# Inverse deviations of the four norms: from chains of small DVE operations to a power operation and a Newton step on Pool

## The chip, the core and the metric

The kernel runs on one core of a Trainium2 chip. The metric is the device time of one execution in microseconds. The core's engines are named as in the profile: PE (matrix multiply; PEld is its weight load), DVE (vector), ACT (scalar, activation functions), POOL (GpSimd), and SP, which here issues DMAs.

## The reference

One decoder layer over 320 tokens: 256 of a prompt and 8 sequences of 8 new tokens each. Cut to what matters:

```python
h = rms_norm(x, norm_mix)                       # norm 1
u, q, k, v, g = split(h @ w_in)
s5_out = s5_mixer(u, ...)                       # complex diagonal state, scanned over positions
o = retention(rotary(q), rotary(k), v, ...)     # 8 heads of 128 channels
mu, var = mean(o, -1), mean(square(o - mu), -1)
o = (o - mu) * rsqrt(var + 1e-6)                # group norm, per head and token
x = x + concat([s5_out, silu(g) * o * ret_gn_w]) @ w_out
h2 = rms_norm(x, norm_ffn)                      # norm 2
x = x + (silu(gate(h2)) * up(h2)) @ w_ffn_out
y = rms_norm(x, norm_final)                     # norm 3
```

`rms_norm` is `x * rsqrt(mean(x * x) + 1e-6) * g`. Outputs are `y` and the new states of both mixers.

## The kernel before

Activations lie with channels on the 128 partitions and the 320 tokens along the row. Every weight tile of 128x1024 is loaded by SP (`raw`), rounded by ACT (`hi`, L128) and its remainder formed by DVE (`lo`, L129), each with three buffers in the mixer; every product is three matmuls of 128x320 (L139 to L141). The norms' scale isn't applied to the matmul's input: the products are taken with the unscaled `x`, and the scale of each token, broadcast to all partitions as `rbc`, is multiplied in when the products leave PSUM.

Three of the four norms go through `rstd_bcast` (L191). PE sums squares over the partitions into `ps_r`, one column for each of three stretches of 128 tokens; DVE brings the sums into `ms` (128x3); `rsqrt` (L181) makes the inverse root `y` of them; and PE broadcasts it with three matmuls against the identity (`ps_r<-ident,ry`, L216), from which ACT copies `rbc`. In norm 1 ACT also copies `ry` itself to `rtok`. In norm 3 PE is kept busy with matmuls on ones (`warm_ps`) during the chain. `rsqrt` was ten DVE operations: a first guess from the bits of the number, then three Newton steps of three operations.

The group norm is in `head_v` (L644): DVE takes mean and variance of `po` in PSUM (`bn_stats`, `bn_aggr`, into `mv` of 128x2x4), then one operation for the variance, the ten of `rsqrt`, and one for the shift: `gy`, scale and shift for four stretches of tokens. ACT applies them to `po` (`on`, L680), and PE transposes `on` into `pn` a while later; in between PE has other matmuls.

The order of work is set in two ways. DVE, ACT and SP are ordered by a scheduler that sees priorities and dependences. PE and Pool are in `manual_schedule`: their instructions stand in the order in which the Python code issues them. That order comes from generators on a model clock: `spawn` puts one in a heap with a due time, `run_due` runs those that are due between matmuls.

What stands on Pool early is the S5 mixer's part: `s5_params` computes step sizes, sines and cosines on DVE (scratch `cl`, result `ecs`), then Pool writes the rotation tables `tab` from `ecs` by doubling, for channel group 0 at once (`s5_tables`, L456) and for groups 1 to 3 as spawned generators. DVE goes on with powers and factors (`lp`, `ff`, `gp`, at last `lx`, all through scratch in `cl`), after which two MEMSETs on Pool clear the two `cl` tiles (L447), since chunks of the mixer use them next. Only after `s5_params` has been issued comes `finish_norm` (L836), which runs `rstd_bcast` for norm 1 in two parts: sums and `rsqrt` first, the broadcast a model delay later, in the midst of the matmuls of head 0's `v`.

## Time and profile before

| what | us |
|---|---|
| median of 3 runs | 1490.53 (1490.41 to 1491.65) |
| the profiled execution's own time | 1490.19 |
| its span, first to last instruction | 1488.4 |
| PE busy | 1462.0 |
| DVE busy | 865.4 |
| ACT busy | 615.1 |
| POOL busy | 77.1 |

In the profile a row of a timeline gives the start in the span, the duration, engine, line, operation and output<-inputs; brackets give how long the engine had been idle before, and what ended that. Where several like instructions follow each other, they are one row (x3) with the time from the first's start to the last's end. A row of the waits gives engine and line, who released it, the total in us, the number of times and the longest. A row of groups gives, after the bar, busy us and the mean ns of one. A row of windows gives the stretch, its length, the busy time in it, granted clock and DMA.

### The profile page before, as it was taken

The page shows a single profiled execution, that of the slowest core. Times are in us where ns is not written, and L with a number is a line of the kernel's source. Part 1 is how long each engine was busy: PE and PEld are TensorE (multiplying, and loading weights), DVE is VectorE, ACT ScalarE, POOL GpSimd, SP SyncE. Part 2 cuts the span into 40 slices and gives each one's busy share as a digit, 9 for nine tenths or more (in the row PEclk, how much of TensorE's full clock was granted, in tenths as well). Part 3 has the DMA queues.
Part 4 walks back from the last instruction along what each step waited for, and adds up shares of the span by engine and source line. Part 5 has one row for each costly group of instructions (what it writes and reads, how often), then busy time and mean ns, then how long its engine had stood idle before and what let it go on. Part 6 is the DMA issues. An engine that isn't in the chain of part 4 may idle for free.

```text
span 1488.4 us, 26179 instructions
## 1 busy us (share of the span) xinstructions
PE 1462.0 (98%) x10558; PEld 1443.7 (97%) x10558; DVE 865.4 (58%) x1507; ACT 615.1 (41%) x980; POOL 77.1 (5%) x159
## 2 busy tenths in 40 slices
PE   9999999999999999999999999999999999999996
PEld 8989999898999999999999999999999999999996
DVE  7988777675746765655444444444444454444454
ACT  6555554554425543333333333333333333333352
POOL 1395000000000000000000000000000000000001
PEclk9999999999999999999999999999999999999999
DMA  7443443433554466665444355444445544445443
GB/s 270 149 140 123 142 142 114 136 121 114 191 163 146 152 210 188 215 221 185 149 149 153 119 155 166 159 149 149 139 137 152 172 153 149 149 123 156 150 145 108
DMA packets 79752, 230.79 MB, mean 155 GB/s; under 512 B 15248, under 2 KB 27664, under 8 KB 79632
## 3 DMA queue, kind: packets, MB, share of 16 engines
q1 hardware_dynamic: 79488, 229.09, 48.2%
q8 instruction: 83, 1.36, 0.4%
q14 instruction: 37, 0.30, 0.1%
q10 hardware_dynamic: 144, 0.04, 0.0%
HBM read 218.04 MB, written 7.63 MB: 152 GB/s over the span
## 4 chain that ended last, share of the span: by engine, by line
PE 68%; DVE 1%; ACT 0%; issue 0%; DVEq 0%
PE ps_fo L139 7%; PE ps_fu L139 7%; PE ps_fu L141 7%; PE ps_fo L140 7%; PE ps_fu L140 7%; PE ps_fo L141 7%; PE ps_fg L139 7%; PE ps_fg L141 7%; PE ps_fg L140 7%; PE ps_o L139 1%; PE ps_o L140 1%; PE ps_o L141 1%; PE ps_g L140 1%; PE ps_g L141 1%; PE ps_g L139 1%; DVE x L174 0%
## 5 line engine op out<-in xcount | busy, mean ns | idle before, releaser
L129 DVE TENSOR_TENSOR lo<-raw,hi 128x1024 fp32r<-128x1024 f32 (+1 forms) x420 | 472.1, 1125 | 393.6 <-ACT hi L128 392.6
L128 ACT CAST hi<-raw 128x1024 fp32r<-128x1024 f32 (+1 forms) x420 | 407.4, 970 | 704.0 <-PE ps_fo L140 188.8
L139 PE MATMUL ps_fg<-hhi,hi 128*128 128x320 f32 x704 | 217.5, 309 | 0.0
L140 PE MATMUL ps_fo<-alo,hi 128*128 128x320 f32 x704 | 217.5, 309 | 0.0
L141 PE MATMUL ps_fo<-ahi,lo 128*128 128x320 f32 x704 | 217.5, 309 | 0.0
L139 PE MATMUL ps_fo<-ahi,hi 128*128 128x320 f32 x704 | 217.5, 309 | 0.0
L141 PE MATMUL ps_fg<-hhi,lo 128*128 128x320 f32 x704 | 217.4, 309 | 0.0
L140 PE MATMUL ps_fu<-hlo,hi 128*128 128x320 f32 x704 | 217.4, 309 | 0.0
L139 PE MATMUL ps_fu<-hhi,hi 128*128 128x320 f32 x704 | 217.4, 309 | 0.0
L141 PE MATMUL ps_fu<-hhi,lo 128*128 128x320 f32 x704 | 217.4, 309 | 0.0
L140 PE MATMUL ps_fg<-hlo,hi 128*128 128x320 f32 x704 | 217.3, 309 | 0.0
L139 PE MATMUL ps_p<-xhi,hi 128*128 128x320 f32 x576 | 183.6, 319 | 0.0
L141 PE MATMUL ps_p<-xhi,lo 128*128 128x320 f32 x576 | 177.9, 309 | 0.0
L140 PE MATMUL ps_p<-xlo,hi 128*128 128x320 f32 x576 | 177.8, 309 | 0.0
L140 PEld LDWEIGHTS ps_fg<-hlo,hi 128*128 128x128 f32 x704 | 132.4, 188 | 0.3
L139 PEld LDWEIGHTS ps_fg<-hhi,hi 128*128 128x128 f32 x704 | 132.3, 188 | 0.3
L139 PEld LDWEIGHTS ps_fo<-ahi,hi 128*128 128x128 f32 x704 | 132.4, 188 | 0.0
L140 PEld LDWEIGHTS ps_fu<-hlo,hi 128*128 128x128 f32 x704 | 132.4, 188 | 0.0
L141 PEld LDWEIGHTS ps_fo<-ahi,lo 128*128 128x128 f32 x704 | 132.4, 188 | 0.0
L141 PEld LDWEIGHTS ps_fg<-hhi,lo 128*128 128x128 f32 x704 | 132.4, 188 | 0.0
L139 PEld LDWEIGHTS ps_fu<-hhi,hi 128*128 128x128 f32 x704 | 132.4, 188 | 0.0
L141 PEld LDWEIGHTS ps_fu<-hhi,lo 128*128 128x128 f32 x704 | 132.4, 188 | 0.0
(414 smaller groups left out, 2003.4 us busy)
## 6 DMA issues: line engine op xcount, KB each, us to landing
raw<-w_fi SPq DMA_DIRECT2D x176, 512.0 KB, 3.7
raw<-w_in SPq DMA_DIRECT2D x76, 512.0 KB, 3.8
raw<-w_fo SPq DMA_DIRECT2D x64, 512.0 KB, 3.5
raw<-w_out SPq DMA_DIRECT2D x32, 512.0 KB, 3.7
raw<-w_fo SPq DMA_DIRECT2D x64, 192.0 KB, 2.4
rt<-r SPq DMA_DIRECT2D x8, 512.0 KB, 4.7
raw<-w_glu SPq DMA_DIRECT2D x8, 512.0 KB, 3.6
raw<-r SPq DMA_DIRECT2D x8, 512.0 KB, 4.4
```

Of the source, the lines that this page charges most:

```text
L128: act.copy(hi[:, :m], raw[:, :m])
L129: dve.tensor_tensor(lo[:, :m], raw[:, :m], f(hi[:, :m]), SUB)
L139: pe.matmul(ps, hi, xhi[:, k], start=k == 0, stop=False)
L140: pe.matmul(ps, hi, xlo[:, k], start=False, stop=False)
L141: pe.matmul(ps, lo, xhi[:, k], start=False, stop=k == nk - 1)
```

## The change

`rsqrt` becomes five Pool operations on the same small tiles: a power (exponent -0.5, from a constant tile `mhalf` filled by a MEMSET at the start), and one Newton step of four. It now takes the variance itself and not its half with a minus sign, so `ms` is scaled by 1/D instead of -0.5/D; that operation stays on DVE. In the group norm the two operations around `rsqrt` go to Pool too and become three: the mean's sign, the addition of epsilon, and the shift. They stand outside the block of high priority now. Per head DVE has 12 operations fewer and Pool 8 more; per norm it is 10 and 5.

```diff
+    mhalf = cst.tile([P, 4], F32, name="mhalf")
+    pool.memset(mhalf, -0.5)
...
     def rsqrt(t, y, tmp):
 
-        ts(y.bitcast(I32), t.bitcast(I32), -0.5, MUL, float(0x1EF759DF), ADD)
-        for _ in range(3):
-            tt(tmp, y, y, MUL)
-            tt(tmp, tmp, t, MUL)
-            stt(y, tmp, 1.5, y, ADD, MUL)
+        pool.tensor_tensor(y, t, mhalf[:, 0:t.shape[1]], ALU.pow)
+        pool.tensor_tensor(tmp, y, y, MUL)
+        pool.tensor_tensor(tmp, tmp, t, MUL)
+        pool.tensor_scalar(tmp, tmp, -0.5, 1.5, MUL, ADD)
+        pool.tensor_tensor(y, y, tmp, MUL)
...
-            ts(ms, ps, -0.5 / D, MUL, -0.5 * EPS, ADD)
+            ts(ms, ps, 1.0 / D, MUL, EPS, ADD)
             if last is not None:
-                stt(ms, sums(last(), "ps_l"), -0.5 / D, ms, MUL, ADD)
+                stt(ms, sums(last(), "ps_l"), 1.0 / D, ms, MUL, ADD)
...
-            ts(mv[:, 1], mv[:, 1], -0.5, MUL, -0.5 * EPS, ADD)
-            rsqrt(mv[:, 1], y[:, 0], y[:, 1])
-            stt(y[:, 1], mv[:, 0], -1.0, y[:, 0], MUL, MUL)
+        pool.tensor_scalar(mv[:, 0], mv[:, 0], -1.0, None, MUL)
+        pool.tensor_scalar(mv[:, 1], mv[:, 1], EPS, None, ADD)
+        rsqrt(mv[:, 1], y[:, 0], y[:, 1])
+        pool.tensor_tensor(y[:, 1], mv[:, 0], y[:, 0], MUL)
```

PE's instructions stand in the same order as before. On Pool, at the end of the first tables, stood before (in brackets the engines whose semaphores an instruction waits for; line numbers are of the kernel before):

```order
L477 TENSOR_TENSOR tab<-tab,ecs 128x8x32
L478 TENSOR_TENSOR tab<-tab,ta 128x8x32 [waits Pool_49]
L447 MEMSET cl_131 128x1280 [waits DVE_49]
L447 MEMSET cl_132 128x1280
L458 MEMSET tab 128x8
L459 MEMSET tab 128x8
L468 COPY tab<-ecs 128x8
```

And now, with the changed kernel's line numbers, where L185 is the power and `ry` and `rt` are norm 1's result and its scratch:

```order
L479 TENSOR_TENSOR tab<-tab,ecs 128x8x32
L480 TENSOR_TENSOR tab<-tab,ta 128x8x32 [waits Pool_49]
L449 MEMSET cl_133 128x1280 [waits DVE_49]
L449 MEMSET cl_134 128x1280
L185 TENSOR_TENSOR ry<-ms,mhalf 128x3
L186 TENSOR_TENSOR rt<-ry 128x3 [waits Pool_49]
L187 TENSOR_TENSOR rt<-rt,ms 128x3 [waits Pool_49]
L188 TENSOR_SCALAR rt<-rt 128x3 [waits Pool_49]
L189 TENSOR_TENSOR ry<-ry,rt 128x3 [waits Pool_49]
L677 TENSOR_SCALAR mv<-mv 128x4 [waits DVE_49]
```

Norm 1's five stand behind the two MEMSETs, and head 0's eight follow them, ahead of the next tables. The later heads' eights stand between the tables of groups 1 to 3, and the last ones after them.

On DVE, where norm 1's broadcast is first used (`csr`, the rotary factors, times `rbc`), stood before:

```order
L129 TENSOR_TENSOR lo<-raw,hi 128x1024 [waits DMAHW0_49,PE_49,Activation_49]
L174 TENSOR_TENSOR csr<-csr,rbc 128x320 [waits DMAHW6_49,Activation_49]
L174 TENSOR_TENSOR csr<-csr,rbc 128x320
L168 TENSOR_SCALAR cl_131<-cl_131 128x96 [waits DVE_49]
L174 TENSOR_TENSOR cl_131<-cl_131 128x96 [waits DVE_49] x2
```

And now:

```order
L176 TENSOR_TENSOR lx_126<-cl_133 128x256 [waits DVE_49]
L176 TENSOR_TENSOR m_959<-raw_bc,gpc 128x512 [waits Activation_49]
L176 TENSOR_TENSOR bl<-m_958,m_959 64x16x16 [waits DVE_49,Pool_49]
L176 TENSOR_TENSOR bl<-m_958,m_959 64x16x16 x3
L176 TENSOR_TENSOR m_966<-raw_bc,lpc 128x512 [waits DVE_49]
L176 TENSOR_TENSOR m_967<-raw_bc,lpc 128x512
L176 TENSOR_TENSOR cl_133<-m_966,m_967 64x4x4x16 [waits DVE_49,Pool_49]
L176 TENSOR_TENSOR cl_133<-m_966,m_967 64x4x4x16 x3
L176 TENSOR_TENSOR csr<-csr,rbc 128x320 [waits DMAHW6_49,Activation_49]
L176 TENSOR_TENSOR csr<-csr,rbc 128x320
```

The use of `rbc` went from the middle of the sine and cosine chain to behind the whole of `s5_params` and behind chunk 0's preparation (`m`, `bl`, `cl`).

## The prediction

> **What bounds the kernel now.** I read the page first, then the waits of PE, then the Pool, DVE and PE timelines around the first norm, and last the tail.

> The page's head and its busy times:

> ```profile
> span 1488.4 us, 26179 instructions
> PE 1462.0 (98%) x10558; PEld 1443.7 (97%) x10558; DVE 865.4 (58%) x1507; ACT 615.1 (41%) x980; POOL 77.1 (5%) x159
> ```

> PE is busy for 98% of the span, so the time is PE's work plus the moments in which it stands. DVE's 126 small instructions that go (10 in each of three norms, 12 in each of eight heads) are worth only what PE waits for them. The waits of PE from 35 to 500 us, with their total, number and longest:

> ```profile
> PE pn L105 <- ACT on L680: 3.9, 4, 1.3
> PE pt L105 <- DVE retp L178: 1.4, 1, 1.4
> PE pst L105 <- DVE cl L174: 1.4, 1, 1.4
> PE pk__1163 L100 <- DVE cl L174: 1.2, 1, 1.2
> PE pn L105 <- ACT bst L533: 0.7, 1, 0.7
> ```

> That is all there is to win in the mixer: 3.9 us behind the group norm, and 4.7 us early on where DVE is crowded. Against this stands what Pool does at that time. Its timeline:

> ```profile
> 53.13 1.23 POOL L468 COPY tab<-ecs 128x8 f32<-128x8 f32 x1 [47.25 <-DVE ecs L174]
> 54.30 0.19 POOL L469 COPY tab<-ecs 128x8 f32<-128x8 f32 x1
> ...
> 67.24 0.73 POOL L478 TENSOR_TENSOR tab<-tab,ta 128x256 f32<-128x256 f32 x1
> 75.67 2.27 POOL L447 MEMSET cl<- 128x1280 f32 x2 [7.70 <-DVE lx L174]
> 77.89 0.11 POOL L458 MEMSET tab<- 128x8 f32 x1
> ```

> Pool stands 47 us for `ecs`, writes the first tables until 67.97, and stands again until the last `lx` lets it clear the `cl` tiles. The next tables' MEMSET and COPY needed nothing but `ecs`, yet did not start in the 7.70 us of that second wait: Pool does what stands first in its queue, and nothing overtakes. The first norm's deviations are wanted much earlier:

> ```profile
> 40.84 0.83 PE L100 MATMUL ps_r<-ident,ry 128*128 128x128 f32 x6
> ```

> PE reaches these broadcast matmuls at 40.84 and, before, waits for nothing. Behind them on PE stands everything else.

> **Part 1, the first norm: a stall.** DVE makes `ms` as before, but the five Pool instructions on it stand in the written order behind the first tables and both MEMSETs of `cl`. So PE waits at `ps_r` for three things: `ecs`, the tables, and the MEMSETs. How early can each be? From DVE's timeline:

> ```profile
> 35.21 0.16 DVE L170 TENSOR_SCALAR ms<-ps_r 128x3 f32<-128x3 f32 x1
> ...
> 42.87 0.89 DVE L174 TENSOR_TENSOR csr<-csr,rbc 128x320 f32<-128x320 f32 x2
> ...
> 52.86 0.21 DVE L174 TENSOR_TENSOR ecs<-cl 128x64 f32<-128x64 f32 x1
> ...
> 75.20 0.41 DVE L174 TENSOR_TENSOR lx<-cl 128x256 f32<-128x256 f32 x1
> ```

> Until 42.87 DVE needs nothing of the norm, and keeps its pace. From there to `ecs` (53.08) and to the last `lx` (75.61) it mixes the parameter chain with work that needs the norm; while PE stands, that work is absent. What the weight splits of L129 take in these two stretches, and the groups that go with them:

> ```profile
> 42.87:53.08 10.21, 2.52 (x3) 1.00 0.41 139
> 53.08:75.61 22.53, 5.12 (x4) 1.00 0.40 123
> ```
> ```profile
> L174 DVE TENSOR_TENSOR u<-pb,rbc 128x320 f32<-128x320 f32 x1 | 0.5, 485 | 0.0
> ```
> ```profile
> L673 DVE BATCH_NORM_STATS2 st<-po 128x6 f32<-128x128 f32 x4 | 1.0, 270 | 0.0
> L174 DVE TENSOR_TENSOR sm<-pss,mk 128x256 f32<-128x256 f32 (+1 forms) x2 | 0.7, 346 | 0.0
> L674 DVE BATCH_NORM_AGGREGATE mv<-st 128x2 f32<-128x6 f32 x4 | 0.7, 163 | 0.0
> L174 DVE TENSOR_TENSOR k__768<-k__768,sw 128x320 f32<-128x320 f32 x1 | 0.5, 480 | 0.0
> ```

> In the first stretch the splits (2.52), the two `csr` (0.89) and five more instructions of that shape (`u` twice, `q_`, `sw`, `q_`; about 0.45 each from one start to the next) move behind the stall: 10.21 - 2.52 - 0.89 - 2.25 = 4.55. Some dependent steps lose the work that filled their gaps; I add 0.5 for it, an estimate. `ecs` is ready at 42.87 + 5.05 = 47.9 instead of 53.08. The tables take 67.97 - 53.13 = 14.84, until 62.8. In the second stretch at least 5.12 + 1.0 + 0.7 + 0.7 + 0.5 = 8.0 of the 22.53 moves away, so the last `lx` is at 47.9 + 14.5 = 62.4 or earlier: the tables end last, though barely. The MEMSETs take 77.89 - 75.67 = 2.22, until 65.0.

> Then the five instructions. No row shows a power operation. Small Pool instructions, free of DVE (first pair) and beside it (second pair, twelve instructions from the one to the other):

> ```profile
> 118.74 0.23 POOL L475 TENSOR_TENSOR tab<-tab,ta 128x16 f32<-128x16 f32 x1
> 119.05 0.22 POOL L476 TENSOR_TENSOR ta<-tab,ecs 128x16 f32<-128x16 f32 x1
> ```
> ```profile
> 78.35 0.40 POOL L473 TENSOR_TENSOR tab<-tab,ecs 128x16 f32<-128x16 f32 x1
> ...
> 84.61 1.34 POOL L473 TENSOR_TENSOR tab<-tab,ecs 128x64 f32<-128x64 f32 x1
> ```

> A dependent step is 0.31 alone, and (84.61 - 78.35) / 12 = 0.52 beside DVE, which here works on chunk 0's `m`, `bl` and `cl`. I take 0.52, so 2.6 for five. The power operation's surcharge I bound by nothing below and by the first COPY above (1.23 against 0.19 for the next: 1.04), and take the middle, 0.5. With 0.1 from Pool to PE, PE goes on at 65.0 + 2.6 + 0.5 + 0.1 = 68.2. The stall is 68.2 - 40.84 = **27.4 us**.

> [...]

> PE also comes back slow. After the waits at the start of its timeline its matmuls step slowly, then at their usual pace:

> ```profile
> 13.74 0.49 PE L823 MATMUL py<-xhi,lo 128*128 128x320 f32 x1 [0.25 <-DVE lo L809]
> ...
> 17.43 0.31 PE L822 MATMUL pb<-xlo,hi 128*128 128x320 f32 x1
> ```
> ```profile
> 20.81 0.31 PE L821 MATMUL pb<-xhi,hi 128*128 128x320 f32 x1
> 20.95 0.31 PE L822 MATMUL pb<-xlo,hi 128*128 128x320 f32 x1
> ```

> From 13.74 to 17.43 are 14 steps in 3.69, which at 0.147 would be 2.06: **1.6 us** more, taken once after the stall; between nothing and twice that.

> What waits behind PE: ACT's copy of `rbc` and all evacuations. When PE goes on, the three weight tiles already split feed it for 3 x 24 steps of 0.147, 10.6 us, so the next loads, which in SP's queue now stand behind the `kst` transfers, come in time: no charge.

> **Part 2, what comes back.** The parameter chain and chunk 0's preparation are done during the stall, and DVE is free afterwards. The four early waits (1.4 + 1.4 + 1.2 + 0.7) should go: **-4.7**. For the group norm, the fifth head's row of the last aggregate and of the last DVE step:

> ```profile
> 255.46 0.18 DVE L674 BATCH_NORM_AGGREGATE mv<-st 128x2 f32<-128x6 f32 x1
> ...
> 264.99 0.16 DVE L178 SCALAR_TENSOR_TENSOR gy<-mv,gy 128x4 f32<-128x4 f32 x1
> ```

> It takes 9.7 us there because larger work comes between the steps. Pool's eight steps at 0.52 and the surcharge are 4.7, and the waits at `pn` were at most 1.3: **-3.9**. Pool's tables of later groups stand between the heads' steps, but none of them waits for anything that comes after its head, so they add nothing.

> **Part 3, the other two norms.** The tail has no cover but the warming matmuls:

> ```profile
> 1474.10 0.17 DVE L170 TENSOR_SCALAR ry<-ms 128x3 int32<-128x3 int32 x1
> ...
> 1475.88 0.16 DVE L178 SCALAR_TENSOR_TENSOR ry<-rt,ry 128x3 f32<-128x3 f32 x1
> 1476.18 0.91 PE L100 MATMUL ps_r<-ident,ry 128*128 128x128 f32 x6
> ```

> Ten DVE steps take 1476.04 - 1474.10 = 1.94. Pool: 5 x 0.31 + 0.5 + 0.1 = 2.15, so **+0.2** (from -0.3 to +1.2). [...] The second norm has FFN matmuls beside it: nothing, or +1.2 if they do not cover (5 x 0.52 + 0.5 against 1.94). The `mhalf` MEMSET (0.11 for its like) hides at the start.

> **The sum.** 27.4 + 1.6 - 4.7 - 3.9 + 0.2 = +20.6 on the profiled execution's 1490.19, which is 1510.8. The median of the runs is 0.34 above that execution: **1511 us**.

> **Rivals.** *Nothing comes back.* The early waits or the group norm's are replaced by others (Pool steps that lose to DVE, evacuations bunched after the stall): 1511 + 8.6 = 1520. For it: DVE is nearly full there. Against it: 8 us of its work and more is done while PE stands.

> *A dear power operation.* At 5 us each, norm one and the tail each gain 4.5, and the head's chain (8 x 0.52 + 5 = 9.2) is as long as DVE's was, so the 3.9 stays: 1511 + 9 + 3.9 = 1524. [...]

> *The other side: no stall.* If Pool reached the five before 40.84, only gains at `pn` were left: 1490.5 - 3.9 + 0.2 = 1487. That needs them ahead of the COPY that waits for `ecs`; the written order has them behind it, and the 7.70 us speak against overtaking.

> **How the numbers follow.** The forecast gets 0.76, nothing comes back 0.14, a dear power operation 0.07, no stall 0.03. The stall's own bounds are 23.8 (tables 2 faster beside less DVE work, steps at 0.31, no surcharge) and 31.8 (`lx` 2 later, all steps blocked). Low end: 23.8 + 1.6 - 8.6 - 0.3 = +16.5, less up to 3 for waits too short to be listed here that a freer DVE may spare: 1504. The high end takes in the first rival with 2 us more: 1522. Left out are the dear power operation, the no-stall case and the thin ends. A measurement of this kernel can tell about 0.2%, 3 us, from no change. Slower has 0.97; the no-stall case splits into faster 0.02 and same 0.01.

> **What would show it.** Right: PE stands from about 41 to 68 at `ps_r`, released by Pool's `ry`; the first tables start near 48; the PE waits of 1.4, 1.4, 1.2 and the 3.9 are gone; the tail from `ms` to `ps_r` is near 2. Wrong: Pool's first `ry` before 41, a stall much under 23 us, a power operation of several us, or new waits of PE between 68 and 400 that add up to more than 4.

## The result and the profile after

The changed kernel takes 1506.22 us (median of 4 runs, 1505.62 to 1507.84), the kernel before beside it 1490.75 us (4 runs, 1490.41 to 1491.65): a ratio of 1.0104, with a 95% interval from 1.0092 to 1.0116. It is slower by about 15.5 us. The forecast was 1511 us, from 1504 to 1522.

The head of the page of the changed kernel, with PE's busy tenths and granted clock in 40 slices:

```profile
span 1504.4 us, 26164 instructions
...
PE 1458.5 (97%) x10558; PEld 1441.7 (96%) x10558; DVE 855.1 (57%) x1381; ACT 613.8 (41%) x980; POOL 102.5 (7%) x239
...
PE   8299999999999999999999999999999999999996
...
PEclk9699999999999999999999999999999999999999
```

The second slice, from 38 to 75 us, is the hole: PE is busy for two to three tenths of it, and its granted clock falls to 0.50 (from 44.07 to 71.38). The longest waits of PE from 35 to 500 us:

```profile
PE ps_r L102 <- POOL ry L189: 27.1, 1, 27.1
PE ps_o L160 <- DVE r4b L176: 0.6, 1, 0.6
```

One wait of 27.1 has come, and the five that the prediction quoted (3.9, 1.4, 1.4, 1.2 and 0.7) are all gone. Pool's timeline up to the release:

```profile
48.12 0.20 POOL L470 COPY tab<-ecs 128x8 f32<-128x8 f32 x1 [42.41 <-DVE ecs L176]
...
60.46 0.95 POOL L480 TENSOR_TENSOR tab<-tab,ta 128x256 f32<-128x256 f32 x1
62.86 2.27 POOL L449 MEMSET cl<- 128x1280 f32 x2 [1.45 <-DVE lx L176]
65.09 1.39 POOL L185 TENSOR_TENSOR ry<-ms,mhalf 128x3 f32<-128x3 f32 x1
...
67.79 0.25 POOL L189 TENSOR_TENSOR ry<-ry,rt 128x3 f32<-128x3 f32 x1
```

Read it from the bottom: norm 1's five steps (65.09 to 68.04) start when the MEMSETs end, the MEMSETs when the last `lx` arrives, 1.45 after the tables end. `ms`, the input of the five, had been there since about 35. DVE's timeline has the two releasers, and the first use of the broadcast:

```profile
47.83 0.23 DVE L176 TENSOR_TENSOR ecs<-cl 128x64 f32<-128x64 f32 x1
...
62.38 0.41 DVE L176 TENSOR_TENSOR lx<-cl 128x256 f32<-128x256 f32 x1
...
70.24 0.89 DVE L176 TENSOR_TENSOR csr<-csr,rbc 128x320 f32<-128x320 f32 x2 [2.25 <-ACT rbc L845]
```

DVE has done the whole parameter chain by 62.79, goes on with chunk 0's preparation, and then itself waits 2.25 for `rbc`. PE's timeline at the resumption:

```profile
68.10 1.65 PE L102 MATMUL ps_r<-ident,ry 128*128 128x128 f32 x6 [27.10 <-POOL ry L189]
...
70.08 0.47 PE L143 MATMUL ps_pv<-xhi,lo 128*128 128x320 f32 x1
...
71.40 0.31 PE L142 MATMUL ps_pv<-xlo,hi 128*128 128x320 f32 x1
```

The duration of one and the same kind of matmul, 0.47 at a granted clock of 0.50 (68.10 to 71.10) and then 0.31 at 0.99 (71.20 to 80.00), shows the slow stretch that follows the stall.

To see where the rest of the time went, I set the starts of the same PE instructions against each other, before and after, in order. The difference grows and shrinks in a few places only (small drifts lie between them, so the last column isn't quite the sum of the rows above):

| place | predicted, us | measured, us | difference after it, us |
|---|---|---|---|
| stall at `ps_r` | +27.4 | +27.3 | +27.3 |
| slow matmuls behind it | +1.6 | +1.6 | +28.9 |
| early waits (`pst`, `pt`, `pk`, head 1's `pn`) | -4.7 | -6.1 | +22.7 |
| `pn` of heads 4 and 6 | -3.9 | -5.8 | |
| `py` behind head 6's `pn`, at full clock now | none | -1.3 | +15.9 |
| tail, and drifts of 0.3 and less | +0.2 | +0.5 | +16.1 |

### The profile page after: what moved, and what is told of

It reads as the page before. It is cut to its first block, busy times and chain, and to the rows that moved or that the text cites. A ratio compares the mean times of both kernels' runs of the same rounds, so it can differ in the third digit from the quotient of the medians.

```text
span 1504.4 us, 26164 instructions
## 1 busy us (share of the span) xinstructions
PE 1458.5 (97%) x10558; PEld 1441.7 (96%) x10558; DVE 855.1 (57%) x1381; ACT 613.8 (41%) x980; POOL 102.5 (7%) x239
## 4 chain that ended last, share of the span: by engine, by line
PE 67%; DVE 0%; POOL 0%; ACT 0%; issue 0%; DVEq 0%; POOLq 0%
PE ps_fo L141 7%; PE ps_fo L142 7%; PE ps_fu L142 7%; PE ps_fu L141 7%; PE ps_fu L143 7%; PE ps_fo L143 7%; PE ps_fg L142 7%; PE ps_fg L141 7%; PE ps_fg L143 7%; PE ps_o L142 1%; PE ps_o L141 1%; PE ps_o L143 1%; PE ps_g L142 1%; PE ps_g L143 1%; PE ps_g L141 1%; DVE x L176 0%
```

## The experiments

The theory: the whole loss is a matter of Pool's queue. Norm 1's five steps, with the broadcast that all of PE waits for, stand behind work that DVE has yet to release; the power operation and Pool's pace are cheap; what the change takes off the group norm is a real gain. The rivals: Pool's steps or the power are dear wherever they stand; nothing comes back; or the gain comes from DVE having less to do, and not from the group norm's shorter way. Each kernel was timed beside the kernel before, which took 1491.06, 1491.05 or 1490.86 us (medians) on those occasions.

### Norm 1 back on DVE, the rest on Pool

```diff
-            rsqrt(ms, y, tmp)
+            (rsqrt_v if tag == "n1" else rsqrt)(ms, y, tmp)
```

`rsqrt_v` is the old chain on DVE, with `ms` scaled as it needs.

> Norm 1 back on DVE with its ten steps, all else as changed. Queue theory: the 27.1 us stall and its 1.6 us of slow matmuls are gone, 5.6 us at the later heads' pn and the 1.2 us of slow matmuls after head 6 stay won; but head 0's eight Pool steps stand behind the two MEMSETs of cl, which in the kernel before waited for lx until 75.67 and ended at 77.89, so PE meets a second stall at head 0's pn (74.25 before, about 81 to 82 now), 6 to 8 us, of which the later early waits give some 4 back: 1487 to 1491. If the place in the queue matters only for norm 1: 1484, no wait at head 0's pn. If Pool's own slowness made the loss: most of it stays, 1500 or more.

Measured: 1490.15 us, a ratio of 0.9993 (0.9984 to 1.0002). So 16 us go with norm 1, but the gain that should have been left over isn't there. The waits of PE say why:

```profile
PE pn L107 <- ACT on L693: 8.0, 1, 8.0
PE pst L107 <- DVE cl L176: 1.4, 1, 1.4
```

And Pool's timeline of that kernel:

```profile
75.36 2.27 POOL L459 MEMSET cl<- 128x1280 f32 x2 [6.97 <-DVE lx L176]
77.60 0.95 POOL L687 TENSOR_SCALAR mv<-mv 128x4 f32<-128x4 f32 x1
...
82.01 0.20 POOL L690 TENSOR_TENSOR gy<-mv,gy 128x4 f32<-128x4 f32 x1
```

Head 0's eight steps stand behind the same two MEMSETs. Without norm 1's stall in front of it, this is a second stall, of 8.0 us, with a slow stretch of PE behind it (granted clock 0.50 from 79 to 89): the difference of PE's starts goes up by 11.75 there, and later gains bring it back to about nothing. In the changed kernel the first stall hid the second.

### Norm 1 alone on Pool

The converse edit: `rsqrt` for norm 1, `rsqrt_v` for the group norm and the other two norms, all where they stood.

> Only norm 1 on Pool; group norm, norm 2 and norm 3 on DVE as before. Queue theory: the same stall of 27 us at ps_r and 1.6 us of slow matmuls after it, the early waits (6.1 us by the comparison of the matmuls' starts) come back, the later pn waits stay as in the kernel before: 1490.7 + 27.1 + 1.6 - 6.1 = 1513. If the many small Pool steps of the group norm made the loss: near 1491.

Measured: 1515.66 us, a ratio of 1.0161 (1.0148 to 1.0175). Norm 1 alone costs 24.6, and the rest of the change gives some 9 of it back. The two longest waits of PE from 35 to 500 us:

```profile
PE ps_r L102 <- POOL ry L189: 27.1, 1, 27.1
PE pn L107 <- ACT on L692: 3.8, 4, 1.3
```

The stall is the same to a tenth, and at `pn` the old waits of the group norm stay. The expected 1513 was 2.7 too low: by PE's starts the slow stretch behind the stall costs 1.2 more here than in the changed kernel, and a second stretch at half the clock (0.53 from 292.00 to 295.40), behind head 4's `pn`, costs another 1.2. So part of those 9 us is the clock's, and not the group norm's way.

### Norm 1's five steps ahead of the tables

Everything on Pool as in the change, but the first tables and the MEMSETs are issued behind norm 1's first part:

```diff
             if g == 0:
-                for _ in s5_tables(ec, es, g):
-                    pass
...
-        for t_ in cls_:
-            pool.memset(t_, 0.0)
...
         next(rg)
+        for _ in s5_tables(ecs[:, 0:NE], ecs[:, NE:], 0):
+            pass
+        for t_ in cls_:
+            pool.memset(t_, 0.0)
```

> The changed kernel with all its Pool operations, but the first tables and the MEMSETs of cl are issued after norm 1's five steps instead of before them. Queue theory: PE finds ry ready at ps_r (Pool's five steps start at about 35.5 and end before 39), no stall there; head 0's steps still stand behind the MEMSETs, so a second stall of 6 to 8 us at its pn as in the kernel with norm 1 on DVE: 1487 to 1491. If Pool's own speed made the loss, it stays near 1506.

Measured: 1491.44 us, a ratio of 0.9999 (0.999 to 1.0008). Pool's timeline around norm 1:

```profile
35.78 0.89 POOL L185 TENSOR_TENSOR ry<-ms,mhalf 128x3 f32<-128x3 f32 x1 [30.15 <-DVE cl L176]
...
37.63 0.24 POOL L189 TENSOR_TENSOR ry<-ry,rt 128x3 f32<-128x3 f32 x1
```

With only the order on Pool changed, the same five instructions are done at 37.87, three microseconds before PE wants them, and no wait at `ps_r` is left. That settles the main question: not the engine, but the place in its queue costs the time. Head 0 then stalls here too, for 7.0 at its `pn`, and takes the gain; an early wait at `pst` is also longer, 2.5 instead of 1.4.

### The MEMSETs alone behind norm 1

The changed kernel with only the MEMSETs moved, so that norm 1 waits for the tables alone.

> The changed kernel with only the two MEMSETs of cl issued behind norm 1's five steps; the first tables stay ahead of them. Queue theory: Pool goes from the end of the tables (61.4) straight to the five steps (about 3.0), so PE goes on at 64.5 instead of 68.1: 3.6 us less, 1502.6. If PE's wait were set by something else on DVE or ACT (the copy of rtok, the parameter chain as such), no change: 1506.2.

Measured: 1500.92 us, a ratio of 1.0064 (1.0051 to 1.0078). Pool's timeline:

```profile
60.94 0.87 POOL L185 TENSOR_TENSOR ry<-ms,mhalf 128x3 f32<-128x3 f32 x1
...
62.72 0.19 POOL L189 TENSOR_TENSOR ry<-ry,rt 128x3 f32<-128x3 f32 x1
67.97 2.28 POOL L840 MEMSET cl<- 128x1280 f32 x2 [5.06 <-DVE lx L176]
```

The five start as the last table ends, and PE resumes at 62.97, 5.1 earlier than in the changed kernel: the five start 4.15 earlier (60.94 against 65.09), and take 1.97 instead of 2.95. So the price of small Pool steps differs with the place as well, for these five by a microsecond; in the changed kernel DVE ran chunk 0's products of `m` and `cl` beside them (65.07 to 68.00).

### PE kept busy during the stall

110 matmuls on ones, whose result isn't used, stand in PE's queue ahead of norm 1's broadcast; then 119.

```diff
+        keep_warm(110)
         rps = next(rg)
```

> The changed kernel with 110 matmuls on ones put on PE between the v projection's first step and the broadcast of norm 1, about 26 us of work that fits into the stall. PE still goes on at 68.1, but its clock is not at half then: the 1.6 us of slow matmuls after the stall are saved, 1504.6. If the slow steps came from waiting weights or the evacuations instead of the clock: 1506.2.

Measured: 1506.06 us, a ratio of 1.0097 (1.0082 to 1.0113), no different from the changed kernel. The fill ended at 66.5, PE still waited 2.3 for `ry`, and the slow steps came all the same: the granted clock was 1.00 from 60.00 to 68.70, the wait included, and 0.50 from 69.70 to 73.10. Two rows of PE's timeline behind the broadcast, 13 steps and 3.44 us apart, which at 0.147 would be 1.9:

```profile
69.71 0.47 PE L142 MATMUL ps_pv<-xlo,hi 128*128 128x320 f32 x1
...
73.15 0.31 PE L143 MATMUL ps_pv<-xhi,lo 128*128 128x320 f32 x1
```

Since the gap wasn't closed, this run can't tell the clock from the rival. The second one closes the gap:

> The changed kernel with 119 instead of 110 matmuls of fill in PE's queue ahead of norm 1's broadcast, so that the gap of 2.3 us behind the fill closes (to under 0.5 us, by 9 more fill matmuls of 0.23 to 0.46 us). Theory 1 (what costs the 1.6 us after the stall is the clock, and a gap of 2.3 us still brought it down): no half-clock stretch between 60 and 80 us, steps at 0.147 from the broadcast on, and about 1504.6 us. Rival (the slow steps come from something else at the start, such as the weight tiles or the loads): the slow steps stay, and about 1506 us.

Measured: 1504.66 us, a ratio of 1.009 (1.0077 to 1.0104). PE's timeline at the same place:

```profile
68.47 0.93 PE L102 MATMUL ps_r<-ident,ry 128*128 128x128 f32 x6 [0.21 <-POOL ry L189]
...
69.68 0.31 PE L141 MATMUL ps_pv<-xhi,hi 128*128 128x320 f32 x1
```

And the window behind it, with the granted clock third from the end:

```profile
69.00:73.00 4.00, 4.00 (x30) 4.00 (x29) 1.77 (x5) 2.13 (x5) 0.00 (x0) 1.00 0.02 4
```

No slow step is left, and the clock is 1.00, against 0.50 with 110. The median is 1.56 below the changed kernel's, but the intervals of the two ratios overlap, so it is the trace that decides. By PE's starts the gain is 1.1 and not 1.6, because norm 1's broadcast starts 0.37 later here (68.47 against 68.10). The slow steps are the clock's, and come from PE's standing: with 2.26 us of it they are there, with 0.21 they are gone.

### Norm 1 and head 0 on DVE, the rest on Pool

```diff
+        if h == 0:
+            with tc.high_priority(offset=GN):
+                ts(mv[:, 1], mv[:, 1], -0.5, MUL, -0.5 * EPS, ADD)
+                rsqrt_v(mv[:, 1], y[:, 0], y[:, 1])
+                stt(y[:, 1], mv[:, 0], -1.0, y[:, 0], MUL, MUL)
+        else:
+            pool.tensor_scalar(mv[:, 0], mv[:, 0], -1.0, None, MUL)
...
```

> Norm 1 and head 0's group norm on DVE, heads 1 to 7 and norms 2 and 3 on Pool: nothing on Pool that stands behind the first tables or the MEMSETs is wanted early. Queue theory: no stall at ps_r and none at head 0's pn; 5.6 us at the later heads' pn and 1.2 us of slow matmuls won, tail +0.2: 1484, faster than both kernels. If the wins of the changed kernel came only from DVE being emptied during the stall: near 1490.5.

Measured: 1482.65 us, a ratio of 0.9942 (0.993 to 0.9955): faster than both kernels. The two things that stood behind the MEMSETs are off Pool, and no wait at any `pn` is left.

### Only heads 1 to 7 on Pool

As the last, and norms 2 and 3 are back on DVE too.

> Heads 1 to 7 on Pool, everything else (norms 1, 2, 3 and head 0) on DVE. Queue theory with the heads as the only gain: the same as with norms 2 and 3 on Pool, 1482.5 to 1483, since norm 3's chain cost 0.2 more on Pool by the trace and norm 2's is covered. If norms 2 and 3 on Pool bring something of their own: above 1484. If they cost: under 1482.

Measured: 1482.27 us, a ratio of 0.9939 (0.9927 to 0.9951). This is the best kernel of the study, and it can't be told from the one with norms 2 and 3 on Pool: those two bring and cost nothing that shows.

### The same, with DVE's load put back

As the last, and DVE also runs the old chain of twelve for heads 1 to 7 at its old place and priority, on a scratch tile whose result isn't used.

```diff
+            with tc.high_priority(offset=GN):
+                dd = mp.tile([P, 4, 4], F32, name="dd", tag="dd", bufs=1)
+                ts(dd[:, 0], st[:, :, 0], 0.0, MUL, -0.5, ADD)
+                rsqrt_v(dd[:, 0], dd[:, 1], dd[:, 2])
+                stt(dd[:, 3], dd[:, 0], -1.0, dd[:, 1], MUL, MUL)
```

> As the kernel with only heads 1 to 7 on Pool (1482.27 us), but DVE also does a chain of twelve operations of the old kind per head, at the old place and priority, on a scratch tile; its result isn't used. So the load on DVE is that of the kernel before (plus nothing), and the way from the variance to the scale and shift is Pool's. Theory 1 (the heads gain because the way to `on` is shorter): no waits at pn, about 1482 to 1484 us. Rival (they gain because DVE has less to do, so that its splits and evacuations come earlier): waits of PE come back, about 1488 to 1490 us.

Measured: 1482.6 us, a ratio of 0.9945 (0.9932 to 0.9959). DVE's instructions on its page, 1507, are as many as in the kernel before:

```profile
PE 1457.8 (98%) x10558; PEld 1440.2 (97%) x10558; DVE 864.6 (58%) x1507; ACT 613.3 (41%) x980; POOL 98.8 (7%) x216
```

The gain stays whole. So the heads gain because the way from the variance to `on` is shorter on an engine with little else to do, and not because DVE is relieved. The longest waits of PE from 100 to 500 us agree, with none at `pn`:

```profile
PE pt L107 <- DVE smp L176: 0.6, 1, 0.6
PE ps_o L160 <- DVE r4b L176: 0.6, 1, 0.6
```

A little of the load does show: this 0.6, one of 1.4 at `pt` and one of 0.4 at `pst` aren't there with only heads 1 to 7 on Pool. Against it stands a slow stretch of PE in that other kernel (1.2 us, granted clock 0.50 from 57.30 to 60.70, shown at the end). A relief of a microsecond or two isn't excluded; the gain at `pn` doesn't hang on it.

### The MEMSETs on DVE

The attempt to save the whole change: norm 1's five first on Pool, then the tables, and the MEMSETs of `cl` on DVE, so that nothing on Pool waits for `lx` ahead of head 0.

```diff
         for t_ in cls_:
-            pool.memset(t_, 0.0)
+            dve.memset(t_, 0.0)
```

> All of the change's Pool operations, but norm 1's five stand ahead of the first tables, and the two MEMSETs of cl are done by DVE, so that nothing on Pool waits for lx. Queue theory: no stall at ps_r; head 0's eight steps start when the first tables end (near 68) instead of behind the MEMSETs (78.8), and PE waits at most about 1 us at head 0's pn: 1483 to 1485. If the second stall came from Pool's steps being slow next to DVE, it stays: about 1490.

Measured: 1488.52 us, a ratio of 0.9981 (0.9973 to 0.999). Head 0's wait is gone, but the time misses the expected one by some 4 us. The longest waits of PE from 35 to 520 us:

```profile
PE pt L107 <- DVE bl L176: 3.2, 1, 3.2
PE pst L107 <- DVE cl L176: 2.3, 1, 2.3
PE pt L107 <- DVE retp L180: 1.0, 1, 1.0
```

These waits add up to 6.5, where the prediction's rows of before have 1.4 + 1.4 + 1.2 = 4.0 early. Only some of it can be the MEMSETs' doing. The wait of 2.3 at `pst` (57.2) and the slow stretch of PE behind it (granted clock 0.50 from 59.10 to 62.50) stand ahead of them (the first is at 74.47); the kernel with the five ahead of the tables has both as well (2.5, and 0.50 from 58.20 to 61.60), with the MEMSETs on Pool. Behind the MEMSETs the two waits at `pt` are 4.2, against 1.4 + 1.2 at `pt` and `pk` before, and a second slow stretch follows (0.51 from 86.40 to 89.80). The MEMSETs take 2.2 us of DVE, and the last `lx` comes 2.3 later than in the kernel before (77.94 against 75.61). That DVE's time for them comes out as PE's wait is argued from this and not shown, and why the wait at `pst` grew stays open.

## Why the prediction was right, and where its sizes were off

**The stall** was right in place, cause and size: 27.3 measured, 27.4 predicted. That the sizes agree to a tenth is partly luck, since its parts were less right than their sum. `ecs` was ready at 48.1 (predicted 47.9); the tables ended at 61.4, not 62.8; and the last `lx` came at 62.79, behind the bound of 62.4, which was to be the latest. Of the tables' 1.5, one is their first COPY, which took 0.20 and not 1.23. In the kernel before it stood beside a weight split on DVE (from 53.09, for 1.22), and in the stall no split is there. So the MEMSETs waited for `lx`, and not, "though barely", for the tables. The MEMSETs' end (65.1 against 65.0) and the five steps with the hop (3.0 against 3.2) then fell about as worked out. The kernel with the five ahead of the tables shows that the place in the queue is the cause. The stall's upper bound, 31.8, counts 2.4 for five steps that are all blocked. No run shows such a term: the five took 2.95 here, 1.97 with the MEMSETs behind them and 2.09 ahead of the tables.

**The slow matmuls** were right: 1.6, and the filled stall of 119 matmuls shows that they are the clock (1.00 there, 0.50 here).

**What comes back** was right in kind and too small, by 1.4 for the early waits and 1.9 for the group norm. This is the mis-sized term, and the reason is the view. I took PE's own idle time. The weight loads stand in a row of their own in the waits, and show more: at the fifth head's `pn` they stood for 0.91 and 1.16, PE by its own row for 0.65 and 0.96. Of the kernel before, from 35 to 500 us:

```profile
PEld pn L105 <- ACT on L680: 5.6, 8, 1.6
PEld pst L105 <- issue: 1.9, 2, 1.7
PEld pt L105 <- issue: 1.6, 1, 1.6
...
PEld pk__1163 L100 <- DVE cl L174: 1.5, 1, 1.5
PEld pn L105 <- ACT bst L533: 0.9, 1, 0.9
```

5.6 at the heads' `pn` and 1.9 + 1.6 + 1.5 + 0.9 = 5.9 early: these are the measured 5.8 and 6.1, nearly. PE's idle time counts from the end of a matmul, 0.31 after its start, though such matmuls otherwise follow each other at 0.147; and half of the eight waits at `pn` don't show on PE at all. The way itself shortened about as worked out, for the fifth head in Pool's timeline:

```profile
278.68 0.36 POOL L677 TENSOR_SCALAR mv<-mv 128x4 f32<-128x4 f32 x1 [44.09 <-DVE mv L676]
...
283.45 0.35 POOL L680 TENSOR_TENSOR gy<-mv,gy 128x4 f32<-128x4 f32 x1
```

These are 5.1 us, against 4.7 predicted and 9.7 on DVE (counted there from the last aggregate).

**The half-clock stretch** was missed altogether. The first matmuls on `xp` behind head 6's `pn`, and the first product behind them, in the kernel before:

```profile
348.72 2.36 PE L100 MATMUL py<-xp,cl 128*32 128x80 f32 x64
...
352.58 0.39 PE L139 MATMUL ps_p<-xhi,hi 128*128 128x320 f32 x1
```

and after:

```profile
365.91 1.31 PE L102 MATMUL py<-xp,cl 128*32 128x80 f32 x64
...
368.51 0.39 PE L141 MATMUL ps_p<-xhi,hi 128*128 128x320 f32 x1
```

The same 64 matmuls took 2.36 and take 1.31; from their start to the product's, the two kernels come 1.3 closer. The windows of the kernel before show the clock:

```profile
348.40:351.90 3.50, 3.50 (x69) 3.05 (x70) 0.65 (x2) 0.68 (x2) 0.00 (x0) 0.51 0.43 150
```

A granted clock of 0.51 stood right behind waits of 1.29 and 0.97 at `pn`. With the waits gone the stretch is gone too: the changed kernel's clock is 1.00 from 71.38 to 1498, and with only heads 1 to 7 on Pool it is 1.00 from 340.00 to 344.00 and from 348.40 to 351.90. With norm 1 alone on Pool it stands (0.52 from 374.00 to 377.40). That it was the waits that brought it is argued from this, from the filled stall, and from the count at the end; it wasn't tried by itself at this place.

**The tail** was put at +0.2 and is nearly nothing: from the first sums to the broadcast 4.39 before (1471.79 to 1476.18) and 4.42 after (1487.87 to 1492.29). The first and last of Pool's five there:

```profile
1490.29 0.85 POOL L185 TENSOR_TENSOR ry<-ms,mhalf 128x3 f32<-128x3 f32 x1 [930.93 <-DVE ms L180]
...
1492.04 0.19 POOL L189 TENSOR_TENSOR ry<-ry,rt 128x3 f32<-128x3 f32 x1
```

They take 1.94, as long as DVE's ten did. From the power's start to the next step's are 0.92, against 0.28 for the dependent steps, so the power's surcharge is about 0.6 here, where DVE runs nothing beside it. That is near the 0.5 that I took, but by luck: one end of the range whose middle I took, the first COPY's 1.04, was the price of the split beside it and tells nothing of a power. The 0.52 a step has such a split in it too: one of its twelve steps, at 80.92, took 1.26 beside a split from 80.88.

**A step that was left out**, without consequence here: in the gaps between the heads' steps the prediction looked only at the tables of later groups ("none of them waits for anything that comes after its head"). Head 0's steps stand behind the MEMSETs, and so wait for `lx`. The kernels with norm 1 on DVE or first in the queue pay 8.0 and 7.0 for it. The prediction looked for the first thing that the MEMSETs delay, and not for the second.

**The rivals.** Nothing coming back and a dear power are refuted by the table and the tail; no run shows a power operation of 5 us, and the longest that was seen took 1.45, at head 0 with norm 1 on DVE. That the stall would not come is refuted for the change as written; but its price, 1487, is what a kernel without either stall was to give, and those with heads 1 to 7 alone on Pool went lower still, to 1482.3, since more went than the 3.9: the loads' share at `pn` (5.6), the slow stretch of 1.3, and early waits of 0.9 at head 1's `pn` and 1.6 at `pt`.

## What to carry to other kernels

A short, urgent chain that moves to an idle engine takes the place that the code's order gives it in that engine's queue (27.1 us of waiting here, none with the order changed): look up what stands ahead of it and what that waits for, and then look for the second and third urgent chain behind the same obstacle, since the first stall hides the others. An engine with hardly any load is a good home for a chain of small dependent steps, because little comes between them; here it halved the way to `on` (5.1 us against 9.7), and the gain stayed when DVE was given its old load back. Read what a wait of PE costs from the rows of the weight loads (5.6 at `pn` here, against 3.9 in PE's own), and count the slow stretch that may follow a wait (1.2 to 1.6 here).

## What the runs showed of the hardware

Some short waits of PE were followed by stretches at half the granted clock: 0.51 behind waits of 1.29 and 0.97 in the kernel before (348.40 to 351.90), 0.50 behind 1.41 with only heads 1 to 7 on Pool (57.30 to 60.70). In the midst of the traces of the kernel before and of the changed kernel these stretches last 3.41 us or a whole number of these (one in the kernel before, from 348.44 to 351.86, and eight, 27.31, at the stall of the changed kernel, from 44.07 to 71.38), and which wait was followed by one was a matter of where it fell. In the kernel with heads 1 to 7 on Pool, PE's timeline around head 0's transposes:

```profile
55.53 0.52 PE L107 MATMUL pst<-ident,k__770 128*128 128x128 f32 x3 [1.41 <-DVE cl L176]
...
58.77 0.47 PE L142 MATMUL ps_p<-xlo,hi 128*128 128x320 f32 x1
```

and in the kernel before:

```profile
55.84 0.52 PE L105 MATMUL pst<-ident,k__768 128*128 128x128 f32 x3 [1.43 <-DVE cl L174]
...
58.72 0.31 PE L139 MATMUL ps_p<-xhi,hi 128*128 128x320 f32 x1
```

```profile
53.91:57.33 3.42, 1.74 (x13) 1.37 (x12) 3.28 (x17) 0.99 (x3) 3.03 (x13) 1.00 0.57 164
```
```profile
54.90:58.31 3.41, 2.20 (x16) 2.04 (x17) 3.24 (x19) 1.26 (x5) 2.94 (x12) 1.00 0.59 166
```

PE stands for 1.68 of the one, and the next step is at half the clock (0.50); it stands for 1.21 of the other, and the next is at full. In the traces of the kernel before and of the changed kernel, from 30 to 1480 us, two steps at full clock were followed by one at half: PE stood for 2.30 of the one (345.03 to 348.44, before) and for 3.07 of the other (40.66 to 44.07, after). Of no other step at full clock did it stand for more than 1.43. It is a count and no experiment; that the standing within one step decides is the author's reading of it, and was not shown. With 110 fill matmuls 2.26 us of waiting were followed by half the clock as well.

The power operation on Pool took 0.85 us on 128x3 with Pool alone (at 1490.29 in the changed kernel), and 1.39 on the same tile beside DVE's products (at 65.09). A dependent Pool step on such a tile took 0.28 from start to start alone (1491.21 to 1492.04), and 0.34 to 0.46 beside those products (66.56 to 67.79). Beside a weight split a step took as long as the split: the one behind the fifth head's power, 128x4 at 280.70, took 1.28 beside a split from 280.71 that took 1.22, like the first COPY of the kernel before (1.23 beside 1.22).
